# A two-layer recurrent trunk on one core: the last head's low parts on VectorE, and a final norm with its sums on every partition

## The chip, the cores and the metric

The kernel runs on one core of one Trainium2 chip. The metric is the device time of one execution in microseconds. Engine names in the profile: PE is TensorE's matmul, PEld its weight load, DVE VectorE, ACT ScalarE, POOL GpSimd, SP SyncE (it only issues DMAs here).

## The reference

A two-layer decoder step over 1024 prompt tokens and 8 x 4 sample tokens, 1056 in all, with 1024 features: an RG-LRU layer, then an HGRN2 layer of 8 heads, each with an input projection, a recurrence, a SiLU gate, an output projection and a residual add. The end of it matters most here:

```python
def _rmsnorm(x, gain):
    xf = x.astype(jnp.float32)
    y = xf * lax.rsqrt(jnp.mean(xf * xf, axis=-1, keepdims=True) + EPS)
    return (y * gain.astype(jnp.float32)).astype(x.dtype)
...
    # second layer, per head: q, f, iv, gate = split(xn @ w_in); chunked recurrence gives o
    y = (o.reshape(Bsz, T, INNER_B) * jax.nn.silu(gate)).astype(x.dtype)
    return x + y @ w_out, S_T.astype(x.dtype)
...
    return _rmsnorm(x, final_gain), ...
```

## The kernel before

Features lie on the 128 partitions and tokens along the free axis; the 1024 features are eight blocks (`KD = 8`) of 128 partitions by 1056 tokens (`TOK`).

**Products.** Each fp32 product is three fp32r matmuls (`mm3`, lines 247 to 249): weights and activations are split into a high part and a low part, and high x high, high x low and low x high are added up in PSUM. A weight's high part is a cast on ScalarE; its low part is the raw weight minus the high part (`subtract`, line 334: on GpSimd, called `G`, or on VectorE, called `V`), or, in most heads, a negated copy on ScalarE and a DMA from GpSimd's queue that accumulates the raw weight onto it (`low`, lines 320 and 321).

**Heads.** The second layer's projections come in a seven-product scheme for 2 x 2 blocks (`seven`): of four raw weight blocks "11", "12", "21" and "22", four `combine` calls (GpSimd, line 1468) make sums in place, and `split(p)` makes the high and the low part for product p. Parts 1 and 2 are split from "11" and "21" before the combines overwrite these slots; parts 6 and 7 are split from the same two slots after them. Head h calls `seven` twice; the last head, h = H - 1 = 7, does not use `low`: parts 1, 2, 6 and 7 are subtracted by GpSimd and parts 3, 4 and 5 by VectorE. Between the products stand bursts of work for the previous and the own head: decays (`scale`, line 1044: VectorE multiplies of two SBUF tensors, with a ScalarE copy, line 1047), masked products, states (line 1245), the copy `os` (ScalarE, line 1249), and `vb` (GpSimd, line 1203).

**Order of work.** Nothing is issued in the order of the text. `Flow` collects the operations of the whole second layer, with the tiles they read and write, planned durations and priorities; it plans forwards and backwards a few times and emits one fixed order for each engine. On each engine an instruction then waits for its semaphores in that order. A change of one operation can so move others anywhere in the layer. In the plan an operation of VectorE that is marked `both` waits for GpSimd's operation of that moment.

**The end.** After the sevens of the output projection, the last two of eight blocks of the contraction (`K2 = 2`) are done for three groups of tokens (`OUT`: 416, 384, 256 columns). For a group and each output block m: six matmuls, an add of the product to `x2[m]` (VectorE, line 1844), a square (ScalarE, line 1846), and a running sum of squares (GpSimd, line 1861), whose last terms are left to TensorE. Before the change the sum over the partitions is made by `norm_sum` (line 283): 128 tokens are the stationary operand and one column of ones moves, so that tokens come to lie on partitions. `roots` adds the terms (lines 1789, 1791, or 1794 for the last group), takes the power -0.5 on GpSimd (line 1796), and builds a diagonal matrix on VectorE (lines 1797, 1801); `spread` (line 1807) multiplies it by ones, so that every partition holds the factors. `finish` multiplies: VectorE does all eight blocks of the first group and five of the others (line 1821), reading the factors in PSUM; ScalarE copies the factors to SBUF (line 1814), scales the other three blocks (line 1818), and GpSimd multiplies them (line 1819). Each block then goes out by a DMA from SP's or ScalarE's queue (line 316). The root of a group is placed at m = `RM` = 3 of the next one, `finish` at m = `SM` = 6; the last group's comes after all products, with twelve filler matmul passes (line 1865) ahead of it.

Of the kernel before, what the change touches and what calls it, by code (L numbers as in the profile page):

```python
# [14 lines left out]
F32 = mybir.dt.float32  # L15
# [3 lines left out]
AF = mybir.ActivationFunctionType  # L19
# [9 lines left out]
HC = 1  # L29
# [2 lines left out]
SPOTS, SPOTS0 = (6, 9, 0, 2), (2, 5, -1, -1)  # L32
LAST = "12b675b43", "12b67b453", "12b675b43", "1b267543"
K2 = 8 - K1
RM, SM, FM, PS = 3, 6, 3, 6
OUT = ((0, 416), (416, 384), (800, 256))

D = 1024
# [177 lines left out]
def tile_trunk(ctx: ExitStack, tc: tile.TileContext, xT, prm, hc, w0, wg, wo0, w1, wo1, s_in,  # L216
# [60 lines left out]
    def spans(n):  # L277
        return [(a, min(128, n - a)) for a in range(0, n, 128)]
# [23 lines left out]
    with ExitStack() as l0:  # L302
# [3 lines left out]
        def fixed(name, shape, dt=F32, pool=None):  # L306
            return (pool or pl).tile(shape, dt, tag=name, name=name)
# [18 lines left out]
        def dve(n, emit, r, w, prio=5, both=False):  # L326
            fl.add("DVE", 0.13 + 0.0011 * n, emit, r, w, prio, both=both)
# [4 lines left out]
        def subtract(e, n, b, x, a, r, w, prio):  # L332

            emit = lambda: e.tensor_tensor(b, x, a.bitcast(F32), op=ALU.subtract)  # L334
            if e is G:
                pool(n, emit, r, w, prio)
            else:
                dve(n, emit, r, w, prio, True)
# [600 lines left out]
    with ExitStack() as l1:  # L939
# [490 lines left out]
        def seven(h, a, b, order, at=()):  # L1430
# [24 lines left out]
            def split(p):  # L1455
                (raw, rk), (hi, hk), (lo, lk) = slot[named[p]], next(his), next(los)
                act(512, lambda: S.copy(hi, raw), (rk,), (hk,), 2)
                if h < H - 1 and ((h, a) != (HC, 0) or p not in BYG):
                    low(512, lo, raw, (rk,), (lk,), 2)
                else:  # L1460
                    subtract(G if p in (1, 2, 6, 7) or h == HC else V, 512, lo, raw, hi, (rk, hk), (lk,), 2)
                parts[p] = hi, lo, (hk, lk)
                if p not in (1, 2):
                    freed.append(slot[named[p]])
# [304 lines left out]
        for o, olds in ((R[:, 0], eight("A", 1)), (SA, [("SA", i) for i in range(2)]), (rows[5], [("vt", i) for i in range(2)]),  # L1769
                        (SG[6], ykeys(0, 0, TOK))):  # L1770
            for a in (0, 512):
                key = ("spare", len(spare))
                inherit(key, olds)
                spare.append((o[:, a:a + 512], key))
        accs, sqs, dgs, sb = cycle(spare[:2]), cycle(spare[2:5]), cycle(spare[5:7]), spare[7]
        nr2 = cycle([(fixed(f"nr2{i}", [128, 4], F32, p1), ("nr2", i)) for i in range(2)])

        def roots(n, sums, ready, groups=1):

            r, rk = next(nr2)  # L1780
            dg, dk = next(dgs)
            f, u = n // 128, n % 128
            dve(4, lambda: V.memset(r, 1.0), (), (rk,), 0)
            srcs = [(slice(i, i + 1), s[:w]) for i, (s, (_, w)) in enumerate(zip(sums, spans(n)))] if groups == 1 else spans(n)
            w = len(srcs)
            if groups > 1:
                view = sums.rearrange("p (g i) -> p i g", i=4)
                for t in ([128, 0, f],) + (([u, f, f + 1],) if u else ()):
                    dve(4, lambda t=t: V.tensor_reduce(r[:t[0], t[1]:t[2]], view[:t[0], t[1]:t[2]], op=ALU.add, axis=mybir.AxisListType.X),
                        ready, (rk,), 0)  # L1790
                dve(4, lambda: V.tensor_scalar(r[:, :w], r[:, :w], 1.0 / D, EPS, op0=ALU.mult, op1=ALU.add), (rk,), (rk,), 0)
            else:
                for q, src in srcs:
                    dve(4, lambda q=q, src=src: V.tensor_scalar(r[:src.shape[0], q], src, 1.0 / D, EPS, op0=ALU.mult, op1=ALU.add),
                        ready, (rk,), 0)
            fl.add("POOL", 0.85, lambda: G.tensor_tensor(r[:, :w], r[:, :w], mhalf[:, :w], op=ALU.pow), (rk,), (rk,), 0)
            dve(128 * f, lambda: V.tensor_tensor(dg[:, :128 * f].rearrange("p (i n) -> p i n", i=f),
                                                 ident[:, None, :].to_broadcast([128, f, 128]),
                                                 r[:, :f, None].to_broadcast([128, f, 128]), op=ALU.mult), (rk,), (dk,), 0)
            if u:  # L1800
                dve(u, lambda: V.tensor_scalar(dg[:, 128 * f:n], ident[:, :u], r[:, f:f + 1], None, op0=ALU.mult), (rk,), (dk,), 0)
            return dg[:, :n], dk

        def spread(n, dg, dk, main):

            bc, bk = next(hg)
            fl.add("PE", 0.002 * n, lambda: T.matmul(bc[:, :n], ones, dg, start=True, stop=True), (dk,), (bk,), 0, main=main)
            return bc[:, :n], bk

        def finish(a, n, bc, bk):  # L1810
            q = slice(a, a + n)
            own = KD - FM if a else KD
            if a:
                act(n, lambda: S.copy(sb[0][:, :n], bc), (bk,), (sb[1],), 0)
            for k in (*range(own, KD), *range(own)):
                x, xk = x2[k][:, q], ykeys(Y2 + k, a, n)
                if k >= own:
                    act(n, lambda x=x, k=k: S.activation(x, x, AF.Copy, scale=pc("gf", k)), xk, xk, 1)
                    pool(n, lambda x=x: G.tensor_tensor(x, x, sb[0][:, :n], op=ALU.mult), (sb[1], *xk), xk, 1)
                else:  # L1820
                    dve(n, lambda x=x, k=k: V.scalar_tensor_tensor(x, x, pc("gf", k), bc, op0=ALU.mult, op1=ALU.mult), (bk, *xk), xk, 1)
                dma(yT[k][:, q], x, xk, (), 1, n / 2, S if k % 2 else Q)

        for a, n in OUT:
            q = slice(a, a + n)
            final = a + n == TOK
            cs = [c for c in range(NCH) if c * CH < a + n and (c + 1) * CH > a]
            acc, ak = next(accs)
            for m in range(KD):
                if a and m == RM:  # L1830
                    dg = roots(prev[1], prev[2], prev[3], KD - PS + 1)
                if a and m == SM:
                    finish(*prev[:2], *spread(prev[1], *dg, True))
                ps, pk = next(mm)
                hi, lo, wk = late[m]

                def emit(ps=ps, hi=hi, lo=lo, q=q, n=n):
                    for k in range(K2):
                        w = slice(128 * k, 128 * k + 128)
                        mm3(ps[:, :n], (hi[:, w], lo[:, w]), yh[K1 + k][:, q], yl[K1 + k][:, q], k == 0, k == K2 - 1)  # L1840

                pe(3 * K2 * n / 2200, emit, (*wk, *((o, K1 + k, c) for o in ("yh", "yl") for k in range(K2) for c in cs)), (pk,))
                x, xk = x2[m][:, q], ykeys(Y2 + m, a, n)
                dve(n, lambda x=x, ps=ps, n=n: V.tensor_tensor(x, ps[:, :n], x, op=ALU.add), (pk, *xk), xk, 0)
                sq, sk = next(sqs) if m else (acc, ak)
                act(n, lambda sq=sq, x=x, n=n: S.activation(sq[:, :n], x, AF.Square), xk, (sk,), 1)
                if final and m >= 4:
                    if m == 4:
                        sums = [(next(hg)) for _ in spans(n)]
                        sumk = [k for _, k in sums]  # L1850
                        sums = [s[:, :1] for s, _ in sums]
                        fl.add("PE", 0.3, lambda acc=acc, n=n, sums=sums: norm_sum(sums, acc, n, True, False), (ak,), sumk, 0)
                    fl.add("PE", 0.3, lambda sq=sq, n=n, m=m, sums=sums: norm_sum(sums, sq, n, False, m == KD - 1), (sk, *sumk), sumk, 0)
                elif m >= PS and not final:
                    if m == PS:
                        s_, sk_ = next(hg)
                        fl.add("PE", 0.5, lambda s_=s_, acc=acc, n=n: norm_sum([s_[:, i:i + 1] for i in range(4)], acc, n, True, True), (ak,), (sk_,), 0)
                    o = 4 * (m - PS + 1)
                    fl.add("PE", 0.5, lambda s_=s_, sq=sq, n=n, o=o: norm_sum([s_[:, o + i:o + i + 1] for i in range(4)], sq, n, True, True), (sk,), (sk_,), 0)
                elif m:  # L1860
                    pool(n, lambda acc=acc, sq=sq, n=n: G.tensor_tensor(acc[:, :n], acc[:, :n], sq[:, :n], op=ALU.add), (sk, ak), (ak,), 1)
            prev = a, n, s_[:, :4 * (KD - PS + 1)], (sk_,)
        spin, wk = next(mm)
        for _ in range(6):
            fl.add("PE", 0.22, lambda: T.matmul(spin[:, :128], ones, ones, start=True, stop=True), sumk, (wk,), 0)
        finish(a, n, *spread(n, *roots(n, sums, sumk), False))
        with tc.manual_schedule(engines={E.PE, E.DVE, E.Activation, E.Pool, E.SP}):
            fl.run()

# [69 lines left out]
```

## Time and profile before

| | us |
|---|---|
| median of 3 runs (1064.13 to 1066.5) | 1064.95 |
| the profiled execution, its own time | 1065.36 |
| its span in the profile | 1063.6 |
| TensorE busy | 1046.8 |
| VectorE busy | 780.2 |
| ScalarE busy | 675.9 |
| GpSimd busy | 510.9 |

The mean granted clock of TensorE is 0.994 of full speed. In a row of the timeline the columns are start, duration, engine, line, operation, tile written <- tiles read, shapes, count, and in brackets the idle time before it on its engine with what ended it. In a table by stage they are the stretch, its length, the busy time with the number of instructions for each engine, the granted clock, the DMA share and GB/s. A row of the waits is: who waited, for whom, microseconds in total, times, longest.

### The profile page before, as it was taken

Reading aid. Unit: us, or ns where it says so; the run is one execution under the profiler, and the core shown is the slowest. Engines: PE = TensorE matmul, PEld = TensorE weight load, DVE = VectorE, ACT = ScalarE, POOL = GpSimd, SP = SyncE. Lnnn points to the kernel's source line nnn. Section 1 sums busy time; section 2 is a strip of 40 time slices with the busy share of each in tenths; the row PEclk is TensorE's granted clock in tenths of the full one; section 3 lists DMA queues with packets and bytes.
Section 4 is the critical chain, followed back from the end, with each engine's and each line's share of the span. In section 5 each row is a group of like instructions: output and inputs, shape, how many; then the busy total and the mean of one; then the engine's idle time right before and its main releaser. Section 6 shows DMA issues by size and latency. Waiting matters only on the chain.

```text
span 1063.6 us, 25952 instructions
## 1 busy us (share of the span) xinstructions
PE 1046.8 (98%) x10120; PEld 1019.3 (96%) x10120; DVE 780.2 (73%) x1528; ACT 675.9 (64%) x1529; POOL 510.9 (48%) x533
## 2 busy tenths in 40 slices
PE   9999999999999999999999999999999989999997
PEld 9999999999999999999999999999999989989996
DVE  7999996888888688265787556556566576999646
ACT  6568656867675874243468685858586745865443
POOL 3425443444533466455455455454445454345454
PEclk9999999999999999999999999999999999999998
DMA  9211112223842695354685564857476752754634
GB/s 300 64 27 45 55 50 74 57 61 108 247 150 61 184 293 160 122 194 144 189 200 118 124 160 104 189 104 168 94 178 132 168 121 84 255 133 111 138 78 164
DMA packets 90763, 143.69 MB, mean 135 GB/s; under 512 B 11152, under 2 KB 56592, under 8 KB 90640
## 3 DMA queue, kind: packets, MB, share of 16 engines
q1 hardware_dynamic: 74656, 112.46, 33.9%
q0 software_dynamic: 13680, 26.81, 14.9%
q10 hardware_dynamic: 2304, 2.77, 0.8%
q8 instruction: 79, 1.29, 0.5%
q14 instruction: 44, 0.36, 0.1%
HBM read 81.60 MB, written 33.05 MB: 108 GB/s over the span
## 4 chain that ended last, share of the span: by engine, by line
PE 87%; DVE 8%; DMA 2%; issue 1%; ACT 0%; POOL 0%; SPq 0%; POOLq 0%; ACTq 0%; DVEq 0%
PE mm L247 24%; PE mm L248 24%; PE mm L249 24%; PE hg L1062 2%; PE hg L1171 1%; PE hg L1279 1%; PE hg L578 1%; PE hg L1281 1%; DVE t L334 1%; PE hg L247 1%; PE hg L248 1%; PE hg L249 1%; PE hg L1225 1%; DVE R L1044 1%; DVE xl L334 1%
## 5 line engine op out<-in xcount | busy, mean ns | idle before, releaser
L247 PE MATMUL mm<-xh,whi 128*128 128x352 f32 (+1 forms) x1147 | 355.2, 310 | 4.2 <-ACT os L1249 3.0
L248 PE MATMUL mm<-xl,whi 128*128 128x352 f32 (+1 forms) x1147 | 349.3, 305 | 0.0
L249 PE MATMUL mm<-xh,wlo 128*128 128x352 f32 (+1 forms) x1147 | 349.1, 304 | 0.0
L247 PEld LDWEIGHTS mm<-xh,whi 128*128 128x128 f32 x1147 | 216.3, 189 | 7.3 <-ACT os L1249 3.2
L248 PEld LDWEIGHTS mm<-xl,whi 128*128 128x128 f32 x1147 | 216.5, 189 | 1.7 <-issue 0.2
L249 PEld LDWEIGHTS mm<-xh,wlo 128*128 128x128 f32 x1147 | 216.4, 189 | 0.0
L334 POOL TENSOR_TENSOR wlo<-wraw,whi 128x512 fp32r<-128x512 f32 (+1 forms) x68 | 97.6, 1443 | 91.0 <-ACT whi L389 74.4
L247 PE MATMUL mm<-t,whi 128*128 128x264 f32 x408 | 119.1, 292 | 0.0
L249 PE MATMUL mm<-t,wlo 128*128 128x264 f32 x408 | 116.8, 286 | 1.0 <-issue 0.9
L248 PE MATMUL mm<-t,whi 128*128 128x264 f32 x408 | 116.6, 286 | 0.0
L510 DVE SCALAR_TENSOR_TENSOR k<-xb,prm_sb,k 128x352 f32<-128x352 f32 (+2 forms) x144 | 90.1, 637 | 10.9 <-ACT k L507 7.7
L249 PEld LDWEIGHTS mm<-t,wlo 128*128 128x128 f32 x408 | 77.4, 190 | 1.4 <-issue 1.1
L247 PEld LDWEIGHTS mm<-t,whi 128*128 128x128 f32 x408 | 77.7, 191 | 0.7 <-ACT k L1518 0.4
L248 PEld LDWEIGHTS mm<-t,whi 128*128 128x128 f32 x408 | 77.6, 190 | 0.1
L1541 DVE TENSOR_TENSOR k<-mm,k 128x264 f32<-128x264 f32 x72 | 30.6, 429 | 55.0 <-PE mm L249 51.4
L321 POOL DMA_DIRECT2D wlo<-wraw x52 | 45.8, 886 | 50.7 <-ACT wlo L320 37.5
L593 POOL TENSOR_TENSOR k<-X 128x352 f32<-128x352 f32 x36 | 45.9, 1282 | 48.0 <-DVE R L594 38.8
L321 POOL DMA_DIRECT2D wlo<-R x32 | 30.0, 937 | 46.6 <-ACT wlo L320 45.0
L389 ACT CAST whi<-wraw 128x512 fp32r<-128x512 f32 (+1 forms) x63 | 36.3, 591 | 21.7 <-DMA wraw<-in_w_dram 11.1
L247 PE MATMUL mm<-yh,whi 128*128 128x352 f32 x153 | 49.9, 326 | 0.0
L249 PE MATMUL mm<-yh,wlo 128*128 128x352 f32 x153 | 49.4, 323 | 0.0
L248 PE MATMUL mm<-yl,whi 128*128 128x352 f32 x153 | 49.4, 323 | 0.0
(427 smaller groups left out, 2715.9 us busy)
## 6 DMA issues: line engine op xcount, KB each, us to landing
wraw<-in_w_dram SPq DMA_DIRECT2D x88, 256.0 KB, 3.2
wlo<-wraw POOLq DMA_DIRECT2D x49, 256.0 KB, 4.0
wlo<-R POOLq DMA_DIRECT2D x30, 256.0 KB, 4.2
wraw<-in_wo_dram SPq DMA_DIRECT2D x37, 192.0 KB, 2.8
ysum<-sg SPq DMA_DIRECT2D x9, 528.0 KB, 4.8
si<-in_s_in_dram SPq DMA_DIRECT2D x8, 512.0 KB, 4.2
R<-in_w_dram SPq DMA_DIRECT2D x16, 256.0 KB, 3.6
out_ss_out_dram<-si SPq DMA_DIRECT2D x8, 512.0 KB, 2.7
```

What stands on the lines that cost most here:

```text
L247: T.matmul(out, wh, xh, start=first, stop=False, skip_group_check=chained)
L248: T.matmul(out, wh, xl, start=False, stop=False, skip_group_check=chained)
L249: T.matmul(out, wl, xh, start=False, stop=last, skip_group_check=chained)
L321: fl.add("POOL", 0.93, lambda: G.dma_start(dst.bitcast(F32), src, accum_op=ALU.add), (*r, *w), w, prio, n / 2)
L334: emit = lambda: e.tensor_tensor(b, x, a.bitcast(F32), op=ALU.subtract)
L389: act(m, lambda hi=hi, raw=raw, m=m: S.copy(hi[:, :m], raw[:, :m]), rk, (hk,), prio)
L510: dve(u, lambda src=src, dst=dst, sh=sh, k=k: V.scalar_tensor_tensor(dst, sh(src, k), pc("cw", 12 * k + m), dst, op0=ALU.mult, op1=ALU.add ...
L578: fl.add("PE", 0.62, lambda ps=ps, i=i, c=c: T.matmul(ps[:96, :CH], gs[:, i, :], ST[:96, chunk(c)], start=True, stop=True), (("gs",), *((" ...
L593: pool(CH, lambda x=x, a=a, b=b: G.tensor_tensor(x, a.bitcast(F32), b.bitcast(F32), op=ALU.add), (ak, bk), (xk,), 3)
L1044: dve(n // 2, lambda sv=sv, dv=dv, s=s, f=f: V.tensor_tensor(dv[:, :, s, :], sv[:, :, s, :], f, op=ALU.mult), (*sk, *gk), dk if i == o els ...
L1062: T.matmul(ps[32 * j:32 * j + 32, n * w:n * w + w], B[:, o:o + 32], q(slice(o, o + 32)), start=True, stop=True, tile_position=(0, 32 * j))
L1541: dve(QT, lambda: V.tensor_tensor(o[0], z[0], u[0], op=ALU.add), (z[1], u[1]), (o[1],), 0)
```

## The change

In `seven`, the last head's parts 1, 2, 6 and 7 are subtracted by VectorE instead of GpSimd. In the final norm, `total` multiplies the squares, as the moving operand, by a 128 x 128 matrix of ones, which accumulates the sums in one PSUM bank with the same sum on every partition. `roots` then takes the square root on ScalarE in that bank, with the scale 1/D and a bias of EPS, and the reciprocal on VectorE in four quarters of the columns. `finish` is as before, but waits for all four quarters, and root and finish of a group both stand at m = 3 of the next one. The last group sums four squares by TensorE as before. `mhalf`'s power, the diagonal, `spread` and the filler matmuls go; the squares' ring has five buffers instead of three.

```diff
-                    subtract(G if p in (1, 2, 6, 7) or h == HC else V, 512, lo, raw, hi, (rk, hk), (lk,), 2)
+                    subtract(G if h == HC else V, 512, lo, raw, hi, (rk, hk), (lk,), 2)
...
+        def total(s, sk, sq, qk, n, start, stop):
+
+            fl.add("PE", 0.00176 * n, lambda: T.matmul(s[:, :n], ones, sq[:, :n], start=start, stop=stop, skip_group_check=True), (qk, sk), (sk,), 0)
+
+        def roots(n, s, sk, more=0.0):
+
+            act(n, lambda: S.activation(s[:, :n], s[:, :n], AF.Sqrt, bias=epsc, scale=1.0 / D), (sk, ("epsc",)), (sk,), 0, more)
+            u = n // 4
+            for i in range(4):
+                w = slice(u * i, u * i + u)
+                fl.add("DVE", 0.11 + 0.0064 * u, lambda w=w: V.reciprocal(s[:, w], s[:, w]), (sk,), ((*sk, i),), 0)
...
         def finish(a, n, bc, bk):
+            more = [(*bk, i) for i in range(4)]
...
-                act(n, lambda: S.copy(sb[0][:, :n], bc), (bk,), (sb[1],), 0)
+                act(n, lambda: S.copy(sb[0][:, :n], bc[:, :n]), (bk, *more), (sb[1],), 0)
...
+            tot, tk = next(hg)
+            own = 4 if final else PS
             for m in range(KD):
                 if a and m == RM:
-                    dg = roots(prev[1], prev[2], prev[3], KD - PS + 1)
-                if a and m == SM:
-                    finish(*prev[:2], *spread(prev[1], *dg, True))
+                    roots(*prev[1:], 0.0 if prev[0] else 1.3)
+                    finish(*prev)
...
+                if m == own:
+                    total(tot, tk, acc, ak, n, True, False)
+                if m >= own:
+                    total(tot, tk, sq, sk, n, False, m == KD - 1)
...
-        spin, wk = next(mm)
-        for _ in range(6):
-            fl.add("PE", 0.22, lambda: T.matmul(spin[:, :128], ones, ones, start=True, stop=True), sumk, (wk,), 0)
-        finish(a, n, *spread(n, *roots(n, sums, sumk), False))
+        roots(*prev[1:])
+        finish(*prev)
```

More of the change, by code (lines that the diff above doesn't have):

```diff
@@ L34 @@
 K2 = 8 - K1
-RM, SM, FM, PS = 3, 6, 3, 6
+RM, FM, PS = 3, 3, 6
 OUT = ((0, 416), (416, 384), (800, 256))
@@ L1774, in tile_trunk @@
                 spare.append((o[:, a:a + 512], key))
[L1775 to L1808, printed above, removed]
+        accs, sqs, sb = cycle(spare[:2]), cycle(spare[2:7]), spare[7]
+        epsc = fixed("epsc", [128, 1], F32, p1)
+        dve(1, lambda: V.memset(epsc, EPS), (), (("epsc",),), 3)
+        def total(s, sk, sq, qk, n, start, stop):
+            fl.add("PE", 0.00176 * n, lambda: T.matmul(s[:, :n], ones, sq[:, :n], start=start, stop=stop, skip_group_check=True), (qk, sk), (sk,), 0)
@@ L1820, in finish @@
                 else:
-                    dve(n, lambda x=x, k=k: V.scalar_tensor_tensor(x, x, pc("gf", k), bc, op0=ALU.mult, op1=ALU.mult), (bk, *xk), xk, 1)
+                    dve(n, lambda x=x, k=k: V.scalar_tensor_tensor(x, x, pc("gf", k), bc[:, :n], op0=ALU.mult, op1=ALU.mult), (bk, *more, *xk), xk, 1)
                 dma(yT[k][:, q], x, xk, (), 1, n / 2, S if k % 2 else Q)
@@ L1846, in tile_trunk @@
                 act(n, lambda sq=sq, x=x, n=n: S.activation(sq[:, :n], x, AF.Square), xk, (sk,), 1)
[L1847 to L1859, printed above, removed]
+                if m == own:
+                    total(tot, tk, acc, ak, n, True, False)
+                if m >= own:
+                    total(tot, tk, sq, sk, n, False, m == KD - 1)
                 elif m:
                     pool(n, lambda acc=acc, sq=sq, n=n: G.tensor_tensor(acc[:, :n], acc[:, :n], sq[:, :n], op=ALU.add), (sk, ak), (ak,), 1)
-            prev = a, n, s_[:, :4 * (KD - PS + 1)], (sk_,)
-        spin, wk = next(mm)
-        for _ in range(6):
-            fl.add("PE", 0.22, lambda: T.matmul(spin[:, :128], ones, ones, start=True, stop=True), sumk, (wk,), 0)
-        finish(a, n, *spread(n, *roots(n, sums, sumk), False))
+            prev = a, n, tot, tk
+        roots(*prev[1:])
+        finish(*prev)
         with tc.manual_schedule(engines={E.PE, E.DVE, E.Activation, E.Pool, E.SP}):
```

## The prediction

> **What bounds the kernel now.** I read the page first (engine shares, chain of waits), then TensorE's waits, then the timeline around each wait that is long, then VectorE's busy time by stage in the tail.
>
> ```profile
> PE 1046.8 (98%) x10120; PEld 1019.3 (96%) x10120; DVE 780.2 (73%) x1528; ACT 675.9 (64%) x1529; POOL 510.9 (48%) x533
> ```
> ```profile
> PE 87%; DVE 8%; DMA 2%; issue 1%; ACT 0%; POOL 0%; SPq 0%; POOLq 0%; ACTq 0%; DVEq 0%
> ```
>
> TensorE carries the span; only its 16.8 idle microseconds, its slow-clock stretches, its norm matmuls and the tail after its last product can be won. The change touches two places: the last head's two sevens (about 866 to 912) and the final norm (from about 1030). Waits there:
>
> ```profile
> PE mm L247 <- ACT os L1249: 3.0, 1, 3.0
> ```
> ```profile
> PE hg L1807 <- DVE sg L1821: 0.7, 1, 0.7
> ```
> ```profile
> ACT a L1047 <- DVE sg L1044: 6.4, 1, 6.4
> ```
>
> The first, TensorE's longest wait of all, falls inside the last head. The timeline of GpSimd, VectorE, ScalarE and TensorE there:
>
> ```profile
> 866.53 1.29 POOL L1468 TENSOR_TENSOR wraw<-wraw,R 128x512 f32<-128x512 f32 x1 [6.42 <-DMA R<-in_w_dram]
> 867.79 1.03 POOL L1203 TENSOR_TENSOR vb<-vst,bm 96x512 fp32r<-96x512 f32 x1
> 868.79 1.26 POOL L334 TENSOR_TENSOR wlo<-wraw,whi 128x512 fp32r<-128x512 f32 x1
> 870.02 1.27 POOL L1468 TENSOR_TENSOR wraw<-wraw 128x512 f32<-128x512 f32 x1
> 871.25 1.29 POOL L334 TENSOR_TENSOR wlo<-R,whi 128x512 fp32r<-128x512 f32 x1
> 872.52 1.25 POOL L1468 TENSOR_TENSOR wraw<-wraw 128x512 f32<-128x512 f32 x1
> 873.72 0.67 POOL L1103 COPY ab<-R 128x32 f32<-128x32 f32 x1
> ```
> ```profile
> 868.80 5.52 DVE L1044 TENSOR_TENSOR sg<-sg 128x512 f32<-128x512 f32 x1
> ```
> ```profile
> 877.34 0.69 DVE L1044 TENSOR_TENSOR R<-R,sg 128x512 f32<-128x512 f32 x1
> ```
> ```profile
> 874.41 0.62 ACT L1047 COPY a<-sg 128x512 f32<-128x512 f32 x1 [6.39 <-DVE sg L1044]
> 875.03 0.27 ACT L1249 COPY os<-mm 128x128 f32<-128x128 f32 x1
> ```
> ```profile
> 875.35 0.39 PE L247 MATMUL mm<-xh,whi 128*128 128x264 f32 x1 [2.95 <-ACT os L1249]
> ```
> ```profile
> 876.00:877.00 1.00, 1.00 (x7) 0.50 0.00 0
> 877.00:878.00 1.00, 1.00 (x6) 0.50 0.00 0
> 878.00:879.00 1.00, 1.00 (x7) 0.50 0.21 62
> ```
>
> Read downward: a VectorE multiply of two SBUF tensors, 0.69 us elsewhere, takes 5.52 us. It starts with GpSimd's subtract at 868.79 and ends 0.6 us after GpSimd's run of two-input operations breaks (the copy at 873.72). ScalarE waits 6.39 us behind it, so its copy of `os`, queued after that one, ends at 875.30, and TensorE, which needs the bank that `os` frees, idles 2.95 us. Then the granted clock (the column after the count) is 0.50 for 3.0 us, losing another 3.0 x 0.5 = 1.5 us. The stall costs 4.45 us.
>
> **Part 1: low parts of the last head to VectorE.** Eight subtracts (parts 1, 2, 6, 7 of two sevens) leave GpSimd, at 1.26 to 1.29 us in the rows above, and become VectorE subtracts of the same shape, near 0.69. Two of them, at 868.79 and 871.25, are what makes GpSimd's run unbroken. After the change GpSimd has only the four combines (L1468) and `vb`. Moreover, the combine into slot "21" overwrites what part 2's subtract reads, and the one into "11" what part 1's reads; both readers now stand in VectorE's queue, so GpSimd must pause for VectorE. Either the multiply goes ahead of the subtract and runs in that pause, or behind it: 868.79 (end of `vb`) + 0.69 + 0.69 is 870.2. ScalarE's two copies end 0.62 + 0.27 later, at 871.1, and TensorE stops only at 875.35 - 2.95 = 872.40. The slack is 1.3 us, so I take the whole 4.45 us as gone. Bounds: 0, if another run starves it as long; 4.45 is all there is.
>
> The new wait, GpSimd's combines on VectorE, has parts 3, 5 and 6 queued behind it. These are covered as long as VectorE's subtracts are earlier than GpSimd's were: part 1's raw weights are there while VectorE is idle, part 2's subtract ends before 872.5, where GpSimd's ended. The run of combines then ends sooner than now, two subtracts having left it. If that cover fails, each late microsecond is one of TensorE. No DMA is moved; raw slots are freed by VectorE instead, which can only change SP's weight loads by the same fraction of a microsecond.
>
> VectorE's cost of the other six: the pair near 900 falls where it waits for products. The pair near 911 falls just ahead of a stretch where it has no room:
>
> ```profile
> 912.00:936.00 24.00, 23.68 (x377) 22.46 (x375) 23.75 (x37) 17.79 (x43) 9.19 (x8) 1.00 0.70 244
> ```
> ```profile
> 913.02 2.20 DVE L1344 TENSOR_TENSOR sg<-sg 128x528 f32<-128x528 f32 x2
> ```
>
> The third busy figure is VectorE's: 23.75 of 24 us. But two additions there take 2.20 instead of 2 x 0.69, while GpSimd's subtracts run; those 0.8 us come back against 2 x 0.69 of new work. Price: 0.6 us of VectorE. TensorE is busy 23.68 us there, so I take 0 and keep 0.6 for the range.
>
> The Trainium skill, "SBUF — State Buffer", section "Who interferes with whom", says a VectorE instruction with two SBUF inputs contends with a GpSimd instruction that reads SBUF, and that whoever issues first holds the port for its whole instruction. By that the multiply should have lost one GpSimd instruction, about 1.3 us, and TensorE nothing; the gain of part 1 would be 0. The rows show a loss of 4.8 us over four instructions, so the trace decides: the loser waits out the run. The rule also speaks against the change, as each moved subtract has two SBUF inputs itself.
>
> **Part 2: the final norm.** Removed: the column sums (L283), the root on GpSimd, the diagonal (L1797, L1801), its spread (L1807) and the filler (L1865). Added: three, three and five matmuls by `ones` over 416, 384 and 256 columns, one ScalarE square root and four VectorE reciprocals per group.
>
> ```profile
> 1032.01 2.54 PE hg L283 x24
> ...
> 1038.93 0.70 PE hg L1807 x2
> ```
>
> TensorE, first group: 2.54 + 0.70 us go, three totals of the spread's shape come, 3 x 0.70. That is 1.1 us less; the second group saves about the same with the 0.7 us wait. So the last product ends about 2 us earlier, but that only matters if VectorE can follow:
>
> ```profile
> 1030.90:1039.70 8.80, 4.90 (x12) 1.00 0.00 1
> 1039.70:1053.86 14.16, 12.45 (x28) 0.99 0.43 158
> 1053.86:1059.50 5.64, 2.47 (x6) 0.73 0.67 235
> ```
>
> VectorE works 19.8 us (4.90 + 12.45 + 2.47) between 1030.9 and its end at 1059.36. Out go these and six smaller ones, of 0.06 to 0.22 us, together 1.0:
>
> ```profile
> 1036.32 0.55 DVE L1797 TENSOR_TENSOR sg<-ident,nr 128x384 f32<-128x384 f32 x1
> ...
> 1037.36 0.86 DVE L1801 TENSOR_SCALAR sg<-ident,nr 128x32 f32<-128x32 f32 x1
> ```
> ```profile
> 1047.13 0.94 DVE L1797 TENSOR_TENSOR sg<-ident,nr 128x384 f32<-128x384 f32 x1
> ```
> ```profile
> 1054.66 0.43 DVE L1797 TENSOR_TENSOR sg<-ident,nr 128x256 f32<-128x256 f32 x1 [0.81 <-POOL nr L1796]
> ```
>
> That is 2.8 + 1.0 = 3.8 us. In come the reciprocals, quarters of 104, 96 and 64 elements. The nearest rows are tiny:
>
> ```profile
> L752 DVE RECIPROCAL smalls<-smalls 128x12 f32<-128x12 f32 x1 | 0.2, 214 | 0.0
> ```
> ```profile
> L785 DVE RECIPROCAL smalls<-smalls 128x8 f32<-128x8 f32 x1 | 0.2, 203 | 0.0
> ```
>
> Low end: their difference, 2.75 ns an element, on a fixed 181 ns: 0.47, 0.45, 0.36 us a quarter, 5.1 us for all twelve. High end: proportional, 214 / 12 = 17.8 ns, over 1056 elements 18.8 us. The ends are far apart; I take their geometric middle, 7 ns, 7.4 us, as the larger part of a 214 ns instruction is surely fixed, yet a division need not stream like an addition.
>
> So VectorE has 19.8 - 3.8 + 7.4 = 23.4 us of work. It still idles before the first reciprocal. The first totals can start where the column sums do now, at 1032.01, and end 2.1 us later, near 1034.1; the root adds:
>
> ```profile
> L597 ACT ACT_TABLE_LOAD  x12: 1283/1283/1283, 83.2 to 392.0; - x12
> L597 ACT ACTIVATE R<-R x12: 1085/1087/1090, 84.5 to 393.3; 128x1056 f32<-128x1056 f32 x12
> ```
>
> taken as 0.55 us for 416 columns (proportionally 0.43), the table's 1.28 us hidden while ScalarE waits for the sum (1.28 us later if not, once). Thus reciprocals start near 1035.1; with two additions like
>
> ```profile
> 1031.00 0.56 DVE L1844 TENSOR_TENSOR ST<-mm,ST 128x384 f32<-128x384 f32 x1 [0.45 <-PE mm L249]
> ```
>
> done by then, VectorE has idled some 4.2 - 1.1 = 3.1 us since 1030.9. From there work never runs out, if the totals come as early as TensorE allows: its end is 1030.9 + 3.1 + 23.4 = 1057.4, against 1059.36. Gain 1.95 us; at the low end 4.2; at the high end a loss of 9.5. The last output leaves now at
>
> ```profile
> 1059.82 0.40 SPq L316 DMA_DIRECT2D out_yT_dram<-a  x1
> ```
>
> and moves with it. GpSimd's three roots are no longer waited for; its share of the outputs is unchanged. `finish` now waits for four reciprocals and stands ahead of additions in VectorE's queue; a late addition holds one of three banks, about two products of cover.
>
> **Sum.** 2.95 + 1.5 + 1.95 = 6.4 us. The profiled execution took 1065.36 us (span 1063.6 and 1.76 around it): 1058.96 after. The median of the runs shown, 1064.95, stands 0.4 lower: 1058.55, say 1058.6.
>
> **Rivals.**
> Starvation stays. Four combines of 1.27 us can still form a run, and VectorE's moved subtracts can meet it. Against: earlier heads have only combines on GpSimd, and the worst loss there is
>
> ```profile
> 756.91 2.65 DVE L1044 TENSOR_TENSOR R<-R,sg 128x512 f32<-128x512 f32 x1
> ```
>
> 2.0 us more than 0.69, against a slack of 1.3. Only the tail then gains: 1064.95 - 1.95 = 1063.0.
>
> VectorE fills the tail. From 9.35 us of reciprocals (8.9 ns an element) on, the tail gains nothing: 1064.95 - 4.45 = 1060.5. For: VectorE is busy 12.45 of 14.16 us already. Against: only the guess of the price. The Trainium skill, "VectorE: DVE Perf Modes", section "First, the fixed hardware budget", says a reciprocal is an iterative division with a repeat count of 8. At the page's 0.96 GHz eight cycles are 8.3 ns, an estimate of 8.8 us for all and of 1060.0 for the kernel; no run here shows it yet.
>
> Slower: the reciprocals alone. From 13.8 us of them (13 ns an element) they eat the whole 6.4; at 17.8 ns the loss is 9.5 - 4.45 = 5.0, 1070. For: VectorE's instructions are on the last chain. Against: 12 elements cost only 11 ns more than 8.
>
> Late low parts: VectorE's full stretch from 912 grows by the 0.6 us, or by 2.8 if all four of the second seven land in it: 1061.4.
>
> **How the numbers follow.** Forecast 0.52; VectorE fills the tail 0.15; late low parts 0.07; starvation stays 0.15; slower 0.07; cheap reciprocals (1056.3) 0.04. What a measurement can tell from no change is about 0.2%, 2.1 us: below 1062.8 is faster. That holds the forecast, two rivals and cheap reciprocals, 0.78, less 0.04 for a changed order of work elsewhere in the second layer, which is planned as one: faster 0.74, same 0.16, slower 0.10. Range: from cheap reciprocals less 0.8 us of such order, 1055.5, to starvation with a poorer tail, 1064.0.
>
> **What would show it.** No L1044 row above 3 us near 868 and no TensorE wait for `os`, with clock 1.00 there: part 1 right. Reciprocal rows near 0.73, 0.67 and 0.45 us, VectorE nearly gapless from 1035 (in today's times) to its end: part 2 right. A new starved VectorE row with TensorE waiting behind it, or quarters above 1 us, would make me wrong.

## The result and the profile after

The changed kernel took 1059.91 us (median of 4 executions, 1059.69 to 1060.73) against 1065.60 for the kernel before beside it (1064.13 to 1066.50): ratio 0.9949, 95% interval 0.9936 to 0.9962. Run again among the last experiments it took 1058.34 against 1064.16, ratio 0.9946, interval 0.9932 to 0.9961. That is 5.7 us less in the first comparison and 5.8 in the second; the forecast was 6.4.

The page of the changed kernel (busy time by engine, then the chain that ended last):

```profile
PE 1038.4 (98%) x10062; PEld 1009.9 (95%) x10062; DVE 781.4 (74%) x1535; ACT 678.6 (64%) x1533; POOL 498.2 (47%) x522
...
PE 88%; DVE 7%; DMA 3%; issue 0%; ACTq 0%; ACT 0%; SPq 0%; POOL 0%; DVEq 0%
```

VectorE's total hardly moved (780.2 to 781.4), although it got eight subtracts and twelve reciprocals, 14 us by their rows: the diagonals and what belonged to them went (3.8 us), and so did the 4.8 us that the one multiply had spent starved, that is, kept waiting beside GpSimd. Where the other 4 us went wasn't taken apart. TensorE is 8.4 us less busy, partly norm matmuls that went, partly time at the full clock.

TensorE's waits in the stretch of the stall (868.7 to 926.5), then GpSimd, VectorE and ScalarE there:

```profile
PE mm L247 <- DVE sg L1541: 0.6, 1, 0.6
```
```profile
867.61 1.28 POOL L1468 TENSOR_TENSOR wraw<-wraw,R 128x512 f32<-128x512 f32 x1 [6.64 <-DMA wlo<-wraw]
868.86 1.57 POOL L1203 TENSOR_TENSOR vb<-vst,bm 96x512 fp32r<-96x512 f32 x1
870.40 2.64 POOL L1468 TENSOR_TENSOR wraw<-wraw 128x512 f32<-128x512 f32 x2
```
```profile
868.85 0.69 DVE L334 TENSOR_TENSOR wlo<-R,whi 128x512 fp32r<-128x512 f32 x1 [2.54 <-PE hg L1062]
...
873.64 1.32 DVE L1044 TENSOR_TENSOR R<-R,sg 128x512 f32<-128x512 f32 x1
...
875.22 1.35 DVE L1044 TENSOR_TENSOR sg<-sg 128x512 f32<-128x512 f32 x1
```
```profile
871.46 0.27 ACT L1249 COPY os<-mm 128x128 f32<-128x128 f32 x1 [2.37 <-PE mm L1233]
```

The 5.52 us multiply is gone. VectorE's moved subtract runs at 868.85 in 0.69 us, and now it is GpSimd's `vb` that stretches (1.57 us instead of 1.03). The copy `os` ends at 871.73 instead of 875.30, since the new plan puts the multiplies behind it (873.64, and at 875.22 the counterpart of the starved one). They take 1.32 and 1.35 us, twice the 0.69 of a free one. Of the 3.0 us wait 0.6 us is left, now for VectorE's addition L1541 (874.88), which stands behind the first of them.

The tail: VectorE's reciprocals (grouped, 1026.76 to the end), the square root with its table, and the stages:

```profile
L1789 DVE RECIPROCAL hg<-hg 128x104 f32<-128x104 f32 x4 | 3.2, 805 | 0.0
L1789 DVE RECIPROCAL hg<-hg 128x96 f32<-128x96 f32 x4 | 3.0, 759 | 0.1
L1789 DVE RECIPROCAL hg<-hg 128x64 f32<-128x64 f32 x4 | 2.3, 563 | 0.1
```
```profile
1029.11 1.28 ACT L1785 ACT_TABLE_LOAD   x1
1030.40 0.58 ACT L1785 ACTIVATE hg<-hg,epsc 128x416 f32<-128x416 f32 x1
```
```profile
1026.76:1035.56 8.80, 8.80 (x46) 7.84 (x45) 5.57 (x10) 5.04 (x8) 3.02 (x3) 1.00 0.00 1
1035.56:1053.70 18.14, 11.01 (x69) 8.77 (x67) 17.89 (x37) 8.81 (x21) 9.25 (x11) 0.93 0.53 192
```

The third busy figure is VectorE's: 17.89 of 18.14 us, nearly gapless to its end.

**A ruler that is finer than the medians.** Executions of one kernel spread over as much as 9 us, but two of its stretches vary less from trace to trace. One runs from the first L1225 matmul of the states of head 5 (heads are counted from 0) to that of head 6 (the stall lies in it; "the head after it" runs from there to head 7's), the other from the first 416-column product to the end of the span. For the kernel before, then the changed kernel:

```profile
867.87 1.83 PE L1225 MATMUL hg<-sg,kt 128*128 128x128 f32 x14
929.60 1.61 PE L1225 MATMUL hg<-sg,kt 128*128 128x128 f32 x12
...
1020.69 0.35 PE L247 MATMUL mm<-xh,t 128*128 128x416 f32 x1
```
```profile
868.77 0.94 PE L1225 MATMUL hg<-sg,kt 128*128 128x128 f32 x6
926.53 2.05 PE L1225 MATMUL hg<-sg,kt 128*128 128x128 f32 x16
...
1016.55 0.35 PE L247 MATMUL mm<-xh,t 128*128 128x416 f32 x1
```

So the stall's stretch went from 929.60 - 867.87 = 61.73 to 57.76 us and the tail from 1063.6 - 1020.69 = 42.91 to 1058.1 - 1016.55 = 41.55. The span fell by 5.5 us: 3.97 in the stall's stretch, 1.36 in the tail, 1.06 in the head after it, less 0.90 that the changed kernel was late at 868. The same rows of every kernel below give:

| kernel | stall's stretch | head after it | tail | median | ratio to before, 95% |
|---|---|---|---|---|---|
| before | 61.73 | 56.30 | 42.91 | | |
| changed | 57.76 | 55.24 | 41.55 | 1059.91 | 0.9949 (0.9936 to 0.9962) |
| e10: changed, again | 58.64 | 55.03 | 41.57 | 1058.34 | 0.9946 (0.9932 to 0.9961) |
| e1: low parts only | 57.66 | 55.65 | 44.42 | 1061.23 | 0.9958 (0.9942 to 0.9973) |
| e2: norm only | 62.90 | 55.94 | 41.57 | 1063.58 | 0.9983 (0.9968 to 0.9997) |
| e3: parts 1, 2 moved | 59.00 | 55.13 | 41.54 | 1060.27 | 0.9949 (0.9930 to 0.9968) |
| e4: parts 6, 7 moved | 61.21 | 54.93 | 41.56 | 1063.09 | 0.9970 (0.9953 to 0.9986) |
| e5: GpSimd filled again | 63.21 | 55.01 | 41.53 | 1062.07 | 0.9969 (0.9955 to 0.9983) |
| e6: ln and exp | 57.44 | 54.82 | 42.76 | 1059.64 | 0.9958 (0.9942 to 0.9974) |
| e7: reciprocals twice | 57.46 | 55.29 | 53.50 | 1071.03 | 1.0063 (1.0038 to 1.0087) |
| e8: one more block | 58.55 | 54.98 | 42.35 | 1060.38 | 0.9959 (0.9945 to 0.9973) |
| e9: mixed roots | 58.25 | 55.47 | 41.75 | 1060.65 | 0.9963 (0.9948 to 0.9978) |

The six kernels that have the changed norm unaltered (the changed kernel twice, e2 to e5) agree in the tail within 0.04 us. Differences of a tail can so be read to 0.1 us, and those of the stall's stretch to about 1 (e10 shows why).

### The profile page after: what moved, and what is told of

Read it like the earlier page. It is cut to its first block, busy times and chain, and to the rows that moved or that the text cites. A ratio compares the mean times of both kernels' runs of the same rounds, so it can differ in the third digit from the quotient of the medians.

```text
span 1058.1 us, 25836 instructions
## 1 busy us (share of the span) xinstructions
PE 1038.4 (98%) x10062; PEld 1009.9 (95%) x10062; DVE 781.4 (74%) x1535; ACT 678.6 (64%) x1533; POOL 498.2 (47%) x522
## 4 chain that ended last, share of the span: by engine, by line
PE 88%; DVE 7%; DMA 3%; issue 0%; ACTq 0%; ACT 0%; SPq 0%; POOL 0%; DVEq 0%
PE mm L247 24%; PE mm L249 24%; PE mm L248 24%; PE hg L1062 2%; PE hg L1171 1%; PE hg L1225 1%; PE hg L1279 1%; PE hg L578 1%; DMA wraw<-in_w_dram 1%; PE hg L1281 1%; PE hg L247 1%; PE hg L248 1%; PE hg L249 1%; DVE t L334 1%; PE hg L1323 1%; DMA sg<-xn 1%
## 5 line engine op out<-in xcount | busy, mean ns | idle before, releaser
L334 POOL TENSOR_TENSOR wlo<-wraw,whi 128x512 fp32r<-128x512 f32 (+1 forms) x62 | 89.8, 1456 | 83.5 <-ACT whi L389 76.4
L1541 DVE TENSOR_TENSOR k<-mm,k 128x264 f32<-128x264 f32 x72 | 30.6, 428 | 49.5 <-PE mm L249 47.2
```

The source lines that it names most:

```text
L1541: dve(QT, lambda: V.tensor_tensor(o[0], z[0], u[0], op=ALU.add), (z[1], u[1]), (o[1],), 0)
```

## The experiments

**e1 and e2: each half alone.** e1 puts the new `split` into the kernel before; e2 puts the old one into the changed kernel.

```diff
# e1, in the kernel before (e2: the reverse, in the changed kernel); arguments shortened
-                    subtract(G if p in (1, 2, 6, 7) or h == HC else V, ...)
+                    subtract(G if h == HC else V, ...)
```

> The kernel before with only the eight low parts moved to VectorE. Theory (GpSimd's unbroken run starves one VectorE multiply, TensorE idles 2.95 us and then runs 3 us at half clock): no wait of TensorE for os near 870, clock 1.00 there, about 4 us less than before, 0.996, give or take 1 us from the new order of the layer. Rival (the gain is all in the final norm): same as before.

> The changed kernel with the low parts of the last head back as before (1, 2, 6, 7 by GpSimd). Theory: the wait of about 3 us for os near 870 and the half clock stay, only the tail is shorter, 1 to 2 us less than before, 0.9985. Rival (the gain is all in the norm): 5 us less than before, 0.995.

e1 took 1061.23 against 1065.58, 4.35 us less: its stall's stretch is 57.66, as in the changed kernel. It would have been more, but its plan of the old norm came out 1.5 us longer in the tail (44.42). e2 took 1063.58, 2.0 us less, and has the tail of the changed kernel (41.57) together with the old stall. Its waits and its multiply:

```profile
PE mm L247 <- ACT os L1249: 3.7, 1, 3.7
```
```profile
870.14 6.26 DVE L1044 TENSOR_TENSOR sg<-sg 128x512 f32<-128x512 f32 x1
```

The halves are separate, and each does what its part of the prediction says.

**e3 and e4: which low parts.** e3 leaves 6 and 7 on GpSimd, e4 leaves 1 and 2 there.

```diff
-                    subtract(G if h == HC else V, ...)
+                    subtract(G if p in (6, 7) or h == HC else V, ...)     # e3; e4: p in (1, 2)
```

> The changed kernel, but parts 6 and 7 of the last head back on GpSimd; only parts 1 and 2, which stand between the combines, by VectorE. Theory (it is these that made the run unbroken): the time of the changed kernel within 1 us, no wait for os. Rival (any four subtracts fewer on GpSimd give their share): half of the gain of the low parts, 2 us slower than the changed kernel.

> The changed kernel, but parts 1 and 2 of the last head back on GpSimd; only parts 6 and 7 by VectorE. Theory: the run of combines and subtracts is unbroken again, a multiply of L1044 above 4 us, TensorE waits for os near 870, about 4 us slower than the changed kernel. Rival (any four subtracts fewer give their share): 2 us slower. Rival (low parts arrive too late for products): no L1044 above 3 us, a wait of TensorE for a low part instead.

Parts 1 and 2 carry it. e3's stretch is 59.00, and its ratio is that of the whole change; e4's is 61.21, with the stall as it was:

```profile
867.14 5.45 DVE L1044 TENSOR_TENSOR sg<-sg 128x512 f32<-128x512 f32 x1
```
```profile
PE mm L247 <- ACT os L1249: 2.9, 1, 2.9
```

By the medians e4 is 2.8 us slower than e3, between the 4 us of the theory and the 2 us of its rival; the trace decides. Half of the move, two subtracts per seven, would have done.

One thing moves along with parts 1 and 2. In the kernel before, in e2 and in e4 the plan has the starved multiply ahead of the copy `os`; in e1, e3 and the changed kernel it has the multiply behind it. No run keeps GpSimd's subtracts and moves only the multiply, so what that order alone would have saved is not shown.

**e5: GpSimd's load without the old dependencies.** VectorE keeps all low parts; GpSimd subtracts parts 1 and 2 once more into a scratch tile that nobody reads.

```diff
+                    if h == H - 1 and p in (1, 2):
+                        pool(512, lambda: G.tensor_tensor(scr, raw, hi.bitcast(F32), op=ALU.subtract), (rk, hk), (("scr",),), 2)
```

> The changed kernel, with GpSimd also subtracting parts 1 and 2 of the last head into a scratch tile that nothing reads; VectorE's subtracts stay. Theory (GpSimd's run is what starves VectorE): a multiply of L1044 of 4 us or more and TensorE's wait for os come back, about 4 us slower than the changed kernel, unless the plan sets the multiply ahead of the run. Rival (what counted was that low parts come from the faster VectorE): as the changed kernel within 1 us.

The stretch is 63.21 us. The wait for `os` that the theory named doesn't come back, as the copy still leaves ahead of the multiplies (869.05). The starved instruction is now the moved subtract itself, and TensorE waits behind it for VectorE:

```profile
866.77 1.03 POOL L1204 TENSOR_TENSOR vb<-vst,bm 96x512 fp32r<-96x512 f32 x1
867.77 1.26 POOL L1464 TENSOR_TENSOR scr<-wraw,whi 128x512 f32<-128x512 f32 x1
869.00 2.95 POOL L1471 TENSOR_TENSOR wraw<-wraw 128x512 f32<-128x512 f32 x2
```
```profile
866.80 4.02 DVE L334 TENSOR_TENSOR wlo<-R,whi 128x512 fp32r<-128x512 f32 x1 [2.90 <-ACT whi L1458]
```
```profile
PE mm L247 <- DVE attns L1070: 2.0, 1, 2.0
PE mm L247 <- DVE sg L1544: 1.8, 1, 1.8
```

So GpSimd's run beside VectorE is enough for a stall, without the old readers of the slots and with the new place of the multiply, and a VectorE low part is not safe in itself.

**m1 and m2: the starving by itself.** Both leave out the whole model. In m1 a GpSimd multiply releases a VectorE multiply of two SBUF tensors, and n more of the same GpSimd multiplies follow without a break; reciprocals are timed at the end. m2 uses the kernel's own forms instead.

```python
# shortened
# m1: n = 0, 1, 2, 4, 6                     # m2: with and without vb
first(); more(n)                            first(); vb; subtract; combine; subtract; combine; small copy
V.tensor_tensor(w, u, v, op=ALU.mult)       V.tensor_tensor(w, u, factors, op=ALU.mult)
```

> No part of the model is computed: a VectorE multiply of two SBUF tensors, 128x512, is released while GpSimd goes through 0, 1, 2, 4 and 6 further multiplies of the same size; then 4 with a small copy between them; then the same with one operand in PSUM, and with one operand only. Then reciprocals of 8 to 416 elements in PSUM and of 12, 64, 416 in SBUF. Theory (the loser waits out the whole run): 0.7 us plus about 1.27 us for each GpSimd multiply, 5.7 us at 4, and half of it with the copy between. Rival (it waits for one instruction only): at most 2 us at any count. Reciprocals: 0.59 at 64, 0.75 at 96, 0.80 at 104 as in the changed kernel, so 6.3 ns an element on 0.15 us, 2.8 us at 416; rival (2.75 ns an element on 0.18 us, from the rows of 8 and 12): 1.3 us at 416.

> Computes no part of the model: a bare run of GpSimd in the kernel's own forms (vb with 96 partitions and broadcast inputs, subtract with a rounded fp32r output, combine in place, subtract, combine, small copy) with VectorE's multiply of two SBUF tensors released beside it. Variants: all of it (twice), without vb, outputs not rounded, nothing in place, a flat instead of a strided multiply, the multiply released later by a ScalarE copy of 64, 256 or 512 columns, two multiplies in a row, and TensorE busy beside it. Theory 'the forms do it': with all of it the multiply takes 3 to 5.5 us as in the kernels, and one variant that leaves out the form that matters takes about 1.7 us. Rival 'the kernel's surroundings do it' (DMA traffic, ScalarE, the moment of release): about 1.7 us in every variant here, as in the plain micro-kernel, or long only where the moment of release or TensorE differs.

m1, VectorE's rows for n = 1 and n = 6, and GpSimd's run of six:

```profile
11.00 1.73 DVE L249 TENSOR_TENSOR w<-u,v 128x512 f32<-128x512 f32 x1 [1.37 <-POOL u L238]
...
24.75 1.73 DVE L249 TENSOR_TENSOR w<-u,v 128x512 f32<-128x512 f32 x1 [4.81 <-POOL u L238]
```
```profile
24.68 7.80 POOL L244 TENSOR_TENSOR b<-q,v 128x512 f32<-128x512 f32 x6
```

1.73 us for n = 1, 2, 4 and 6, against 0.67 for n = 0: VectorE lost one GpSimd instruction and then got in, and GpSimd's run grew to 7.80 us. By m1 my mechanism was false. m2 shows what was missing. VectorE's second and third multiply, with GpSimd's runs beside them:

```profile
16.10 6.39 DVE L272 TENSOR_TENSOR w<-u,gg 128x512 f32<-128x512 f32 x1 [1.41 <-POOL u L278]
23.87 1.73 DVE L272 TENSOR_TENSOR w<-u,gg 128x512 f32<-128x512 f32 x1 [1.38 <-POOL u L278]
```
```profile
16.02 1.04 POOL L251 TENSOR_TENSOR vb<-vst,bm 96x512 fp32r<-96x512 f32 x1
17.02 1.26 POOL L256 TENSOR_TENSOR lo<-r,hi 128x512 fp32r<-128x512 f32 x1
...
21.89 0.65 POOL L268 COPY gg<-bm 128x8 f32<-128x8 f32 x1
22.57 1.26 POOL L278 TENSOR_TENSOR u<-w,q 128x512 f32<-128x512 f32 x1
23.79 1.26 POOL L256 TENSOR_TENSOR lo<-r,hi 128x512 fp32r<-128x512 f32 x1
25.01 1.71 POOL L259 TENSOR_TENSOR r<-r,r 128x512 f32<-128x512 f32 x1
```

With `vb` first, the multiply waits out all five instructions and gets in at the small copy, as in the kernel. Without `vb` the same subtracts and combines cost it 1.73 us. Unrounded outputs, no combine in place, a flat multiply, a later release by ScalarE and a busy TensorE all left it at 5.74 to 6.39. The starved rows around the last head fit, and one in an earlier head: each (868.80, 756.91 before; 870.14 in e2; 867.14 in e4; 866.80 in e5; 867.70, 2.61 us, in e3; 868.01, 2.80 us, in e8; 867.99, 2.49 us, in e9; 865.88, 2.63 us, in e10) began its wait within `vb` or less than 0.1 us after it. In e3 and e5 the subtract got in between two combines in a row, the second of which has to wait, by the program, for VectorE's subtract of part 1; the trace shows a gap of 0.08 us there (868.49 + 1.26 to 869.83 in e3). At the other boundaries one instruction begins before the row of the last has ended. One row of the changed kernel doesn't fit: a multiply took 3.72 us in head 1, begun beside a DMA issue of GpSimd, with no `vb` ahead:

```profile
583.82 3.72 DVE L1044 TENSOR_TENSOR sg<-sg 128x512 f32<-128x512 f32 x1
```
```profile
583.66 0.88 POOL L321 DMA_DIRECT2D wlo<-R  x1
```

So `vb` is not the only instruction that can open such a wait. Which property of `vb` matters (96 partitions, its broadcast inputs, its shorter time) is open; it wasn't tried.

**e7: reciprocals twice.** Each quarter is inverted twice, so that the factor is the root itself: 8.5 us more of VectorE's work in the tail.

```diff
                 fl.add("DVE", 0.11 + 0.0064 * u, lambda w=w: V.reciprocal(s[:, w], s[:, w]), (sk,), ((*sk, i),), 0)
+                fl.add("DVE", 0.11 + 0.0064 * u, lambda w=w: V.reciprocal(s[:, w], s[:, w]), (sk,), ((*sk, i),), 0)
```

> The changed kernel with each reciprocal done twice, so that the factor is the root and not its reciprocal: 8.6 us more of VectorE's work in the tail. Theory (VectorE has no idle time from 1031 on): 8 us slower than the changed kernel. Rival (reciprocals lie beside other work): only the last group's four count, 2.3 us.

The tail grew by 53.50 - 41.55 = 11.95 us, more than the added work, since additions that come late hold TensorE's banks:

```profile
PE mm L247 <- DVE sg L1828: 4.6, 1, 4.6
PE mm L247 <- DVE R L1828: 1.8, 1, 1.8
```

**e6, e8, e9: less for VectorE in the tail.** e6 takes all factors on ScalarE as exp(-0.5 ln(.)), e9 only those of the first two groups; e8 gives ScalarE and GpSimd a fourth block (`FM = 4`).

```diff
-            act(n, lambda: S.activation(s[:, :n], s[:, :n], AF.Sqrt, bias=epsc, scale=1.0 / D), ...)
...
-                fl.add("DVE", 0.11 + 0.0064 * u, lambda w=w: V.reciprocal(s[:, w], s[:, w]), ...)
+            act(n, lambda: S.activation(s[:, :n], s[:, :n], AF.Ln, bias=epsc, scale=1.0 / D), ...)
+            act(n, lambda: S.activation(s[:, :n], s[:, :n], AF.Exp, scale=-0.5), ...)
...
```

> The changed kernel with the reciprocal square root of the final norm by ScalarE as exp of -0.5 times ln, without VectorE's reciprocals (8.6 us of VectorE's work). Theory (VectorE's work bounds the tail from about 1031 on): the end comes earlier, bounded next by TensorE's last totals, about 3 us less than the changed kernel; if ln and exp need a table load each time, 1.28 us of it per load goes again. Rival (the tail hangs on the chain sum, root, factors): no change or slower.

> The changed kernel with the factors of groups 1 and 2 taken on ScalarE as exp(-0.5 ln(mean + eps)), those of the last group by root and reciprocals. VectorE loses 4 x 0.82 + 4 x 0.77 = 6.4 us in the tail, ScalarE gets two more table loads of 1.28 us and two passes of 0.5 us. Theory 'VectorE bounds the tail': 1.5 to 3 us below the changed kernel, about 1057.5. Rival 'the bound moves to ScalarE's queue, with squares behind table loads and TensorE's totals behind the squares': no gain over the changed kernel (1059.6 to 1060.5), with a TensorE wait for a square or a sum of 1 us or more.

> The changed kernel with FM = 4: in groups 2 and 3 four blocks instead of three are scaled by ScalarE and multiplied by GpSimd, so VectorE has 0.60 + 0.47 us less in the tail. Theory 'VectorE's work sets the end of the tail': 0.5 to 1.0 us below the changed kernel, 1059.0 to 1059.5. Rival 'the last products and ScalarE's or GpSimd's part set it': no change or 0.7 us more (GpSimd's product of 0.73 us is the last to end).

None shortens the tail: 42.76, 41.75 and 42.35 against 41.55. The medians (ratios 0.9958, 0.9963, 0.9959) are not below the changed kernel's; e6's profiled span of 1055.0 came from an early start of its tail. In e9 VectorE has 12.93 of 17 us of work where the changed kernel has 16.65, yet it waits for ScalarE:

```profile
1036.80:1053.80 17.00, 9.49 (x60) 7.74 (x58) 12.93 (x28) 11.57 (x22) 7.26 (x9) 0.91 0.53 190
```
```profile
1049.10 2.37 DVE L1790 RECIPROCAL hg<-hg 128x64 f32<-128x64 f32 x4 [0.52 <-ACT hg L1786]
```

TensorE's wait for a square there is 0.8 us, where the rival had 1 or more. In e6 the squares stand behind two table loads per group, and TensorE waits 2.1 us for a running sum made of them:

```profile
PE hg L1781 <- POOL R L1832: 2.1, 1, 2.1
```

In e8 VectorE ends 0.08 us earlier, but GpSimd's last product (1053.06, 0.72 us) 0.5 us later, and the span 0.8. The tail of the changed kernel is level: VectorE sets its end (e7), but once VectorE is relieved, ScalarE's queue (e9) or GpSimd (e8) sets an end that is 0.2 or 0.8 us later.

**e10: the changed kernel again**, for a comparison on the same chip.

> The changed kernel, unaltered, for direct comparison on the same chip: 1059.9 against 1065.4, ratio 0.995; if the earlier result was luck of the chip, 0.997 to 0.998.

Ratio 0.9946. No version beat it. Its trace shows what the first one hid:

```profile
865.70 1.03 POOL L1203 TENSOR_TENSOR vb<-vst,bm 96x512 fp32r<-96x512 f32 x1
```
```profile
865.88 2.63 DVE L334 TENSOR_TENSOR wlo<-R,whi 128x512 fp32r<-128x512 f32 x1 [2.58 <-ACT whi L1457]
```

The kernel is the same, but here `vb` began 0.18 us ahead of the moved subtract, which took 2.63 us. In the first trace the subtract began 0.01 us ahead of `vb` (868.85 and 868.86), took 0.69 us, and `vb` stretched. The traces with parts 1 and 2 moved and GpSimd not filled again fall in two groups by this. With the subtract first (changed, e1, e6, e7: 0.69 to 0.87 us) the stall's stretch is 57.4 to 57.8 us; with `vb` first (e3, e8, e9, e10: 2.49 to 2.80 us) it is 58.2 to 59.0. So about 1 us of the stretch goes with which of the two starts first.

## Why the prediction was right, by its steps

- **What bounds, and the stall (right).** Taking parts 1 and 2 off GpSimd removes the `os` wait near 870 and its slow clock (TensorE's clock is 1.00 from 860 to 920); putting them back, in e2 or e4, or the load alone, in e5, brings the loss back.
- **Part 1, 4.45 us (right, a little large).** The stretch gave 3.97 us, and 3.1 in e10. What I left out is the wait that is late next: TensorE waits 0.6 us for VectorE's L1541 addition, in e10 1.0 for it and 0.3 for `attns`. 4.45 less these is 3.85 and 3.15, close to the two measured figures. Both waits stand behind rows that were kept waiting: in the changed kernel the addition follows the multiply of 1.32 us, and in e10 VectorE works almost without a break from the subtract of 2.63 us on. The path was another than I wrote. A slip of mine lies in it, and in the description of the kernel: part 2 is split from slot "12", not "21" (part 7 is), so only the combines into "11" and "12" wait for VectorE's subtracts, and these come last. The plan also moved the multiply behind the copy. The copy ended at 871.73, which is 870.8 in the times of before and near the 871.1 reckoned, but it waited for TensorE and not for the multiply.
- **"The loser waits out the run" (right here, wrong as a rule).** In m1 the loser loses one instruction; with `vb` ahead it loses all of them. The Trainium skill, "SBUF — State Buffer", section "Who interferes with whom", which I set aside, says that the holder keeps the port for its instruction: m1's 1.73 us agrees, m2's 6.39 us with `vb` does not. Had the run been of subtracts and combines alone, that rule would have been the better guide: by m2's 1.73 us without `vb` the multiply would have lost 1 us. The rival "starvation stays" is real in e5, at 4.02 us, and in the changed kernel itself, at 2.63 us in e10, with TensorE's 1.3 us behind it: a row of the kind that I had named as a sign of being wrong, though small enough to leave most of the gain. That the first trace had none was luck of 0.01 us.
- **VectorE's price in the second seven, 0 with 0.6 kept (sign wrong).** Around 912 to 936 (909 to 933 after, 3 us earlier) VectorE's work fell:

```profile
909.00:933.00 24.00, 24.00 (x385) 23.21 (x384) 21.54 (x38) 18.67 (x44) 7.29 (x7) 1.00 0.71 240
```

  21.54 us instead of 23.75, with more instructions (38 against 37): its additions L1344 there now take 0.70 each. TensorE has no idle time where it had 0.3. The head after the stall is 1.06 us shorter, 1.27 in e10, which I had not counted; e1 has 0.65 of it and e2 0.36. TensorE's waits make up 0.7 of the 1.06: before, 0.9 us at 951.60, for which the profile shows no releaser, and 0.3 for `attns`; after, 0.5 for L1541. The first wait stands in e1, e2 and e3 too (0.8, 0.9, 0.8), so it isn't this execution's alone. Why it goes in the changed kernel wasn't taken apart.
- **Part 2, 1.95 us (right, a little large).** The tail gave 1.36. VectorE's end came 1.54 us earlier against its first 416-column product, but what follows its last multiply took 4.42 us instead of 4.24. Its idle time was 3.5 us where I had 3.1, as the first reciprocal came behind an addition that waited for TensorE (1031.55, or 1035.7 in the times of before, not 1035.1). The work was 5.57 + 17.89 = 23.46 us where I had 23.4, by luck: two errors cancel. The reciprocals took 4 x (805 + 759 + 563) ns = 8.5 us instead of 7.4, and the rest came out 1.1 us lower. The same 34 additions and multiplies stand in both tails; after the change they follow one another without gaps, and such rows overlap (1051.64 + 0.47 beside the next start at 1052.03), which makes up most of the 1.1. The Trainium skill's repeat count for a reciprocal ("VectorE: DVE Perf Modes", "First, the fixed hardware budget") gave 8.8 us as an estimate, nearer than my middle of 7.4. The guess between two tiny rows mis-sized this term; with it alone put right, the sum would have left 0.85 us of the 1.95. The table load was hidden (1029.11, ahead of the sum), as assumed.
- **The sum.** 3.97 + 1.36 + 1.06 - 0.90 = 5.5 us in the profiled executions. The 0.90 before 868 comes with a wait for `os` of 1.5 us in head 1, behind the multiply of 3.72 us at 583.82. e10, the same kernel, does not have it (e9 does): chance of that execution, but starving of the same kind.

## What to carry to other kernels

A starved instruction is found by its duration (5.52 us against 0.69), not by a wait of its own, and it is worth asking which instruction of the other engine began the run: parts 1 and 2 mattered here, 6 and 7 did not. Two traces of one kernel are worth comparing at such a place, since hundredths of a microsecond decided there which engine starved. Before moving work onto an engine, take its per-element price from a few-line kernel rather than from rows of 8 and 12 elements. Where a tail has three engines within a microsecond of each other, relief for one of them buys nothing, and a fixed pair of rows in the trace tells that where medians can't.

## What the runs showed of the hardware that was not expected

- A VectorE multiply with two SBUF inputs takes 1.73 us beside 1, 2, 4 or 6 back-to-back GpSimd multiplies (0.67 with none), and 6.39 us, through all five instructions, when `vb` (96 partitions, broadcast inputs) stands first.
- In these traces the instruction that began first won: the moved subtract took 0.69 us when it began 0.01 us ahead of `vb`, and 2.63 us when it began 0.18 us behind it.
- In m1, beside four GpSimd multiplies, an instruction with one SBUF input was slowed as well, 1.47 us instead of 0.43, and one whose second operand is in PSUM was not:

```profile
L258 DVE TENSOR_SCALAR w<-u 128x512 f32<-128x512 f32 x1 | 1.5, 1472 | 5.4 <-POOL u L238 5.4
L255 DVE TENSOR_TENSOR w<-u,ps 128x512 f32<-128x512 f32 x1 | 0.7, 687 | 5.0 <-POOL u L238 5.0
L265 DVE TENSOR_SCALAR z<-w 128x512 f32<-128x512 f32 x1 | 0.4, 427 | 0.0
```

- A VectorE reciprocal costs 6.25 ns an element on 0.166 us, by m1's rows in PSUM:

```profile
L262 DVE RECIPROCAL ps<-ps 128x416 f32<-128x416 f32 x1 | 2.8, 2766 | 0.0
L262 DVE RECIPROCAL ps<-ps 128x64 f32<-128x64 f32 x1 | 0.6, 566 | 0.0
```

  (2766 - 566) / 352 = 6.25 ns; 566 - 64 x 6.25 = 166 ns.
